# Hybrid decoder step: the linear attention's decay products on GpSimd ahead of the levels, with the order of all engines written out

## The chip, the cores and the metric

One core of a Trainium2 chip runs the whole step in one launch. Its engines work side by side, each on its own queue in order: TensorE (PE, matmuls, with weight loads listed as PEld), VectorE (DVE), ScalarE (ACT), GpSimd (POOL) and SyncE (SP), which issues the DMA transfers. The metric is the device time of one launch in microseconds; lower is better.

## The reference

A one-layer decoder step for a prompt of 2048 tokens and for 64 sample tokens (8 sequences of 8). One input projection feeds two mixers and their gates; the output projection is added to the residual. Mixer A is sliding-window attention in three windows and dilations, for the prompt and, with a cache, for the sample. Mixer B is gated linear attention with 4 heads, key size 64 and value size 128:

```python
def step(state, xs):
    qc, kc, vc, gc = xs
    b = jnp.cumsum(gc, axis=2)
    diff = b[:, :, :, None, :] - b[:, :, None, :, :]
    decay = jnp.exp(jnp.where(causal[:, :, None], diff, -jnp.inf))
    scores = jnp.einsum('bhtk,bhsk,bhtsk->bhts', qc, kc, decay)
    o = (jnp.einsum('bhts,bhsv->bhtv', scores, vc)
         + jnp.einsum('bhtk,bhkv->bhtv', qc * jnp.exp(b), state))
    b_last = b[:, :, -1]
    state = (jnp.exp(b_last)[..., None] * state
             + jnp.einsum('bhsk,bhsv->bhkv', kc * jnp.exp(b_last[:, :, None] - b), vc))
    return state, o
```

`gc` is the logarithm of a forget factor for each token, head and key channel. A score between two tokens carries the product of the factors between them.

## The kernel before

The prompt is cut into 16 tiles of 128 tokens. Each is normalised, transposed and multiplied by the input weights, block of columns by block of columns (`acc_q`, `acc_k`, `acc_v`, `acc_qkb`, `acc_g`, `acc_vb`, `acc_gb`; inputs and weights are split into two float16 parts, and each 128 rows of the weights take three matmuls). The windowed attention runs beside the projections. Then come the linear attention, while the last block of columns (`acc_gb`, the gate of mixer B) is still projected, and the output projection `Y`, beside which the sample's attention over the cache (`OS`) runs to the end.

The linear attention of the prompt works in eight blocks of 256 tokens (`e0` to `e7`; two chunks of 128 in each), one of the sample (`smp`) before them. `gla_core` does one block. Keys and queries are transposed to channels on partitions (`kq_e`: `kT` and `qT`, 128 x 2 x 256 numbers, flattened to 512 columns `k` and `q`), and so are the forget factors, `d_e`. Scores are then made by doubling: at level B (1, 2, 4, 8, 16, 32, 64; for the sample the first three) each pair of neighbouring spans of B tokens gets the scores of its later queries against its earlier keys. For that the later queries must carry the decay from the start of their span and the earlier keys the decay to the end of theirs. One level is:

- ACT copies the later queries into a zero-padded tile `qbd` (three tiles in turn, L840), PE makes the score products `sc_e` (L881; at level 64 L865), and VectorE writes them under a mask into `Ac_e` (L887);
- `decay()` then multiplies the earlier keys by the later span's whole factor on GpSimd (L848) and the later queries by the earlier span's whole factor on VectorE (L852). After it, every span of 2B tokens is decayed as one;
- the whole factors of the doubled spans, needed by the next level, are the products of neighbours (L858), half as many at each level: 256, 128, 64, 32, 16, 8 and 4 columns for a block of the prompt.

The keys of a level can only be decayed when the level's score products have read them, and the next level's products need the decayed keys: a chain of PE and GpSimd. The queries make a second one of ACT and VectorE. The last product of a block, the decay over a whole chunk, is read again by the state's update (`Sbd`, L1940). The tiles `d` and `sums` have two buffers each.

Around it on VectorE stand the normalisation of the outputs (`oss_c`, `rv_o_c`, `ra_o_c`, `ors_c`), the gate (`so_gb`, L1303 and L1311) and the mixing with the windowed attention (`oc`, `mn`, `mix`, `mt`); on GpSimd `prod_e`, `Ac_e` (L789), `gw` (L1395), `oc` (L2149) and the sample's dot products `pr` (L1616).

The order of each engine's instructions is fixed before the launch. A class `Plan` reads all instructions, finds their dependencies, prices each, and makes a list schedule by priorities; two tables of numbers in the kernel then change some priorities (`steps`) and move some rows (`shifts`). The result is given to the framework as the order in which each engine must run; the framework adds the semaphores.

Of the kernel before, what the change touches and what calls it, by code (L numbers as in the profile page):

```python
# [51 lines left out]
class Plan:  # L52

    ENGINES = ("PE", "DVE", "Activation", "Pool", "SP")

    def __init__(self, tc, nc, cross=35.0, traffic=1.0, lanes=8, room=212832):

        self.tc, self.cross, self.traffic = tc, cross, traffic
        self.lanes, self.room = lanes, room
        self.window, self.least = 3413.0, 0.5  # L60
        self.turns = ((0.0, 93.0, 93.0), (93.0, 0.0, 195.0), (93.0, 60.0, 0.0))
        traced = nc.cur_bb.bb.instructions
        self.at = {i.name: n for n, i in enumerate(traced)}
        self.ins = [
            i for i in traced
            if type(i).__name__ not in ("BassTilePoolBoundary", "InstTileManualSchedule")
        ]
        self.eng = [str(i.engine).split(".")[-1] for i in self.ins]
        self.bits, self.pools = {}, {p.id: p for p in tc.info.pools}
        self.read()  # L70
        self.depend()
        self.price()

    def mask(self, ap, dims, nbytes, row):

        key = (tuple(dims), ap.offset, nbytes, row)
        m = self.bits.get(key)
        if m is not None:
            return m

        def places(start, dims):
            idx = [start]
            for step, n in dims:
                if n > 1 and step:
                    idx = [i + step * j for j in range(n) for i in idx]
            return idx

        m = 0
        if row:
            p0, col = divmod(ap.offset, row)  # L90
            last = col + sum(step * (n - 1) for step, n in dims[1:])
            lo, hi = col * nbytes // 4, (last * nbytes + nbytes - 1) // 4
            line = (1 << (hi + 1)) - (1 << lo)
            width = row * nbytes // 4 + 1
            for q in range(p0 // 32, (p0 + dims[0][1] - 1) // 32 + 1):
                m |= line << (q * width)
        else:
            dims, run = list(dims), 1
            while dims and (dims[-1][0] == run or dims[-1][1] == 1):
                run *= dims.pop()[1]  # L100
            span = (1 << ((run + 15) // 16)) - 1
            for e in set(places(ap.offset, dims)):
                m |= span << (e // 16)
        self.bits[key] = m
        return m

    def read(self):

        self.acc, self.tile = [], {}
        for i in self.ins:  # L110
            acc = []
            for aps, w in ((i.ins, False), (i.outs, True)):
                for a in aps:
                    ap = getattr(a, "bass_ap", None)
                    if ap is None or getattr(ap.tensor, "cap_key", None) is None:
                        continue
                    t = ap.tensor
                    size = {F16: 2, BF16: 2}
                    nbytes = size.get(a.dtype, 4)
                    row = 0  # L120
                    if t.space != DRAM:
                        row = 1
                        for s in list(t.shape)[1:]:
                            row *= s
                        row = row * size.get(t.dtype, 4) // nbytes
                    m = 1 if t.space == PSUM else self.mask(
                        ap, [tuple(x) for x in a.ap], nbytes, row
                    )
                    acc.append((t.name, w, m))
                    self.tile.setdefault(t.name, t)  # L130
            if type(i).__name__ == "InstCopyPredicated":
                acc += [(t, False, m) for t, w, m in acc if w]
            self.acc.append(acc)

    def spans(self):

        end = len(self.at)
        events = []
        for p in self.pools.values():
            if p.space == DRAM:  # L140
                continue
            a = self.at[p.alloc_inst.name]
            r = p.release_inst and self.at.get(p.release_inst.name)
            events.append((a, 1, p))
            if r:
                events.append((r, 0, p))
        events.sort(key=lambda e: e[:2])
        stacks, slots = {}, {}
        for at, opens, p in events:
            st = stacks.setdefault((str(p.space), str(p.side)), [])  # L150
            if not opens:
                st[:] = [s for s in st if s[0] != p.id]
                continue
            lo = top = max((s[1] for s in st), default=0)
            for tag, meta in p.tag_meta.items():
                size = (meta.max_size_bytes // P + 31) // 32 * 32
                for j in range(meta.bufs):
                    slots[f"{tag}_{p.name}_{p.id}", j] = (str(p.space), str(p.side), top, top + size)
                    top += size
            st.append((p.id, top))  # L160
        for k, (space, side, lo, hi) in slots.items():
            if "right" in side.lower():
                lo, hi = self.room - hi, self.room - lo
            slots[k] = (space, lo, hi)
        return slots

    def depend(self):

        slots = self.spans()
        dep = [set() for _ in self.ins]  # L170
        behind = [set() for _ in self.ins]
        gates = []

        def gate(before):
            before = frozenset(before)
            if before:
                gates.append(before)
                return {len(self.ins) + len(gates) - 1}
            return set()

        whole = {}
        for n, acc in enumerate(self.acc):
            for t, _, _ in acc:
                whole.setdefault(t, []).append(n)

        of_pool, room = {}, {}
        for t, tile in self.tile.items():
            if tile.space != DRAM:
                of_pool.setdefault(str(tile.tag).rsplit("_", 1)[1], []).append(t)
        for (key, _), (space, lo, hi) in slots.items():  # L190
            i = key.rsplit("_", 1)[1]
            sp, l0, h0 = room.get(i, (space, lo, hi))
            room[i] = space, min(lo, l0), max(hi, h0)
        opens = {}
        for p in self.pools.values():
            i = str(p.id)
            if i not in room:
                continue
# [12 lines left out]
        for n, acc in enumerate(self.acc):  # L211
            for t, w, m in acc:
                if t in hist:
                    continue
# [2384 lines left out]
```

## Time and profile before

| | us |
|---|---|
| three runs: median (lowest to highest) | 1244.23 (1243.79 to 1245.26) |
| profiled execution, its own time | 1242.09 |
| its span, from first to last instruction | 1240.2 |
| PE busy | 1188.2 (96%) |
| VectorE busy | 947.9 (76%) |
| ScalarE busy | 820.6 (66%) |
| GpSimd busy | 545.1 (44%) |

The granted TensorE clock was 0.999 of full speed on the mean. Busy times of engines overlap. A row of a group gives its line, engine, operation, tiles, sizes and count, then its busy time and the mean of one in ns, then the idle time of the engine just before it and what ended that. "A <- B" in a table of waits means that A stood still until B was done. The ends of matmuls are modelled, so a gap of a few hundredths of a microsecond on PE isn't seen.

### The profile page before, as it was taken

To read this page: it belongs to the slowest core of one execution; us is meant where nothing else is said; L and a number is where in the kernel's file an instruction comes from. 1 tells how busy PE (TensorE), PEld (TensorE's weight loads), DVE (VectorE), ACT (ScalarE), POOL (GpSimd) and SP (SyncE) were. 2 spreads that over 40 slices of the span, in tenths; PEclk is the share of its full clock that TensorE was granted. 3 is DMA by queue.
4 is the path that set the end of the run, shared out by engine and by line. 5 is a ranking of instruction groups with operands and counts; after the bars stand their busy time and mean duration, and the time that the engine had idled before them with its cause. 6 is when DMAs were issued, how large, how long until landed. Compare 5 with 4: busy or idle time off the path is not lost.

```text
span 1240.2 us, 26200 instructions
## 1 busy us (share of the span) xinstructions
PE 1188.2 (96%) x8942; PEld 716.7 (58%) x8942; DVE 947.9 (76%) x2450; ACT 820.6 (66%) x2191; POOL 545.1 (44%) x475
## 2 busy tenths in 40 slices
PE   5999999999999999999999999999999999999998
PEld 3444564666566556666677665545655665555543
DVE  7988788988898958668677665589999999833662
ACT  6554697889689968968767653568878864411220
POOL 0154442575647334552444466655635454501220
PEclk9999999999999999999999999999999999999999
DMA  8668947986856898789999886865772477899971
GB/s 298 231 172 237 241 131 167 245 226 184 203 169 164 213 250 282 229 245 248 257 260 256 247 229 212 231 196 174 233 249 95 156 245 235 279 379 349 399 267 49
DMA packets 235831, 283.07 MB, mean 228 GB/s; under 512 B 116193, under 2 KB 146866, under 8 KB 232626
## 3 DMA queue, kind: packets, MB, share of 16 engines
q1 hardware_dynamic: 235698, 281.40, 75.8%
q8 instruction: 71, 1.16, 0.4%
q14 instruction: 62, 0.51, 0.1%
HBM read 183.02 MB, written 75.24 MB: 208 GB/s over the span
## 4 chain that ended last, share of the span: by engine, by line
PE 51%; DVE 19%; DMA 9%; ACT 8%; issue 5%; POOL 5%; SPq 1%; POOLq 0%; DVEq 0%; ACTq 0%
PE Y L2107 10%; PE acc_qkb L1761 4%; PE acc_gb L1761 4%; PE acc_v L1761 3%; PE t L1052 3%; PE acc_k L1761 3%; PE s L1034 3%; POOL pr L1616 3%; PE O L1067 3%; PE acc_q L1761 3%; PE acc_g L1761 2%; PE acc_vb L1761 2%; DMA k<-in_cache_k_win 2%; PE OS L2364 2%; DVE p L1042 2%
## 5 line engine op out<-in xcount | busy, mean ns | idle before, releaser
L1616 POOL TENSOR_TENSOR pr<-k,qb 128x512 f32<-128x512 f32 x128 | 168.3, 1315 | 171.1 <-DVE sck L1617 70.2
L1761 PEld LDWEIGHTS <-hr 128*128 128x128 f16 x1824 | 172.5, 98 | 110.9 <-issue 11.1
L1045 ACT ACTIVATE p<-p,o 128x256 f32<-128x256 f32 (+1 forms) x384 | 173.1, 455 | 22.9 <-DVE o L1042 20.2
L1761 PEld LDWEIGHTS <-hl 128*128 128x128 f16 x1248 | 119.7, 98 | 118.6 <-issue 7.0
L2107 PE MATMUL Y<-w_o,mh 128*128 128x512 f16 x768 | 180.4, 379 | 0.1
L1067 PE MATMUL O<-v,pt 128*128 128x128 f16 x1200 | 135.1, 220 | 7.9 <-DVE pt L1015 2.6
L1019 POOL TENSOR_TENSOR pt<-p,pt 128x512 f16<-128x512 f32 (+1 forms) x80 | 91.1, 1138 | 116.5 <-ACT pt L1018 92.0
L1617 DVE TENSOR_REDUCE sck<-pr 128x8 f32<-128x512 f32 x128 | 87.1, 680 | 56.7 <-POOL pr L1616 56.5
L1052 PE MATMUL t<-ident,p 128*128 128x128 f32 x600 | 119.2, 279 | 5.5 <-ACT p L1045 3.0
L2107 PEld LDWEIGHTS <-mh 128*128 128x128 f16 x768 | 72.3, 98 | 79.0 <-issue 5.6
L1067 PEld LDWEIGHTS <-pt 128*128 128x128 f16 x1200 | 94.6, 99 | 39.9 <-DVE pt L1015 4.6
L1761 PE MATMUL acc_v<-w_v,hl 128*128 128x512 f16 x384 | 110.0, 383 | 1.1 <-DVE vp L1416 1.0
L1761 PE MATMUL acc_g<-w_g,hr 128*128 128x272 f16 (+1 forms) x768 | 109.3, 276 | 1.4 <-DVE so_g L1303 1.4
L1761 PE MATMUL acc_q<-w_q,hl 128*128 128x512 f16 x384 | 109.5, 379 | 0.5 <-DVE vp L1416 0.5
L1761 PE MATMUL acc_k<-w_k,hl 128*128 128x512 f16 x384 | 108.7, 379 | 0.9 <-DVE vp L1416 0.9
L1761 PE MATMUL acc_vb<-w_vb,hr 128*128 128x512 f16 x384 | 95.3, 379 | 0.3 <-DVE so_g L1303 0.3
L1042 DVE CUSTOM_DVE_ANT_0 p<-s,m3w,scl_s 128x128 f32<-128x128 f32 (+1 forms) x256 | 87.2, 395 | 9.0 <-PE s L1034 5.1
L1761 PE MATMUL acc_gb<-w_gb,hr 128*128 128x512 f16 x384 | 93.8, 380 | 0.0
L1052 PEld LDWEIGHTS t<-ident,p 128*128 128x128 f32 x600 | 74.2, 141 | 28.4 <-ACT p L1045 14.1
L1034 PE MATMUL s<-kk,qq 128*128 128x256 f16 (+1 forms) x512 | 84.7, 264 | 4.4 <-DVE o L1042 2.3
L1761 PE MATMUL acc_qkb<-w_qkb,hr 128*128 128x512 f16 x288 | 81.5, 379 | 1.5 <-ACT zq L1381 1.5
L2149 POOL TENSOR_TENSOR oc<-oc 128x512 f32<-128x512 f32 x32 | 40.1, 1270 | 88.4 <-DVE oc L2142 69.4
(538 smaller groups left out, 2502.2 us busy)
## 6 DMA issues: line engine op xcount, KB each, us to landing
k<-in_cache_k_win SPq DMA_DIRECT2D x104, 256.0 KB
sv_b<-in_cache_v_win SPq DMA_DIRECT2D x24, 1024.0 KB
hr<-h_d SPq DMA_DIRECT2D x44, 512.0 KB
qb<-q_d SPq DMA_DIRECT2D x64, 256.0 KB
oc<-o_d SPq DMA_DIRECT2D x48, 264.0 KB
o_d<-o SPq DMA_DIRECT2D x64, 132.0 KB
x<-in_x_prompt SPq DMA_DIRECT2D x16, 512.0 KB
h_d<-hl SPq DMA_DIRECT2D x16, 512.0 KB
```

Source lines behind the costliest of these rows:

```text
L1019: POOL.tensor_tensor(l, f, h, ALU.subtract)
L1034: PE.matmul(s_ps[:, i * w : (i + 1) * w], q, k, start=(n == 0), stop=(n == len(prods) - 1),)
L1042: DVE.tensor_tensor_reduce(s[:, sl], s_ps[:, sl], mask, neg, BIG, ALU.add, ALU.min, nmf(i))
L1045: ACT.activation(s[:, sl], s[:, sl], AF.Exp, bias=nmf(i), scale=-1.0, accum_out=denf(i))
L1052: PE.transpose(p_ps[:, i * P : (i + 1) * P], t["s"][:, i * P : (i + 1) * P], ident[:])
L1067: PE.matmul(o_, t["pt"][:, c, (i * nb + b) * P : (i * nb + b + 1) * P], vf(i, b), start=(n == 0), stop=(n == 2 * nb - 1),)
L1616: POOL.tensor_tensor(pr[:], kt, qt, ALU.mult)
L1617: DVE.tensor_reduce(out, pr[:].rearrange("p (u k d) -> p u k d", u=2, k=4), AX.X, ALU.add)
L1761: PE.matmul(z, a_[:, k, :], w[:, p_, k, cols], start=(k == 0 and i == 0), stop=(k == KT - 1 and i == 2),)
L2107: PE.matmul(Y[:], a_[:, k, :], w_[:, part, k, :512], start=(i == 0), stop=(i == len(prods) - 1),)
L2149: eng.tensor_tensor(o_[g], o_[g], w[:, g].unsqueeze(2).to_broadcast([P, NH, HD]), ALU.mult)
L2364: PE.matmul(OS[32 * x : 32 * x + 32, 0:256], ps(x), vs_[bb][:, 256 * u : 256 * u + 256], start=(i == 0), stop=(i == 13),)
```

## The change

In `gla_core` the products of neighbours leave `decay()`. They are made by GpSimd instead of VectorE, and all levels of a block are made in one loop, before the first level's copy of queries; `wholes` keeps them, and level number `li` reads `wholes[li]`. The numbers computed are the same.

```diff
         sums = gt.tile([P, 2 * n], F32, name=f"sums_{tagp}", tag="sums", bufs=2)
-        whole, free = d[:], 0
+        wholes, free = [d[:]], 0
+        for B in levels:
+            M = n // B
+            part = wholes[-1].rearrange("p (m two) -> p m two", two=2)
+            wholes.append(sums[:, free : free + M])
+            free += M
+            POOL.tensor_tensor(wholes[-1], part[:, :, 0], part[:, :, 1], ALU.mult)
 
         yield
         for li, B in enumerate(levels):
...
-            part = whole.rearrange("p (m two) -> p m two", two=2)
+            part = wholes[li].rearrange("p (m two) -> p m two", two=2)
 
             def decay():
-                nonlocal whole, free
                 POOL.tensor_tensor(
                     kv[:, :, 0, :], kv[:, :, 0, :], part[:, :, 1:2].to_broadcast([P, M, B]),
                     ALU.mult,
                 )
...
-                whole = sums[:, free : free + M]
-                free += M
-                DVE.tensor_tensor(whole, part[:, :, 0], part[:, :, 1], ALU.mult)
...
-        return qT, kT, whole.rearrange("p (a m) -> p a m", a=2), Ac
+        return qT, kT, wholes[-1].rearrange("p (a m) -> p a m", a=2), Ac
```

The class `Plan` and the tables `steps` and `shifts` are removed. In their place stands, for each engine, the list of its instructions' numbers (as they are written in the program) in the order in which they run:

```diff
+ORDER = {
+    "PE": (
+        "6-7 0 2-4 1 5 10-25 8-9 74 90-91 75 92-93 76-77 94-99 78 100-113 79-89 26-33 42-49 34-41 50-65 "
...
+def in_order(tc, nc):
+
+    traced = {e: [] for e in ORDER}
+    for i in nc.cur_bb.bb.instructions:
+        if type(i).__name__ not in ("BassTilePoolBoundary", "InstTileManualSchedule"):
+            traced[str(i.engine).split(".")[-1]].append(i)
+    info = mybir.DependencyInfo(mybir.DependencyClass.NoSync, mybir.DependencyReason.DATA)
+    for e, runs in ORDER.items():
+        ends = [[int(n) for n in r.split("-")] for r in runs.split()]
+        order = [traced[e][n] for r in ends for n in range(r[0], r[-1] + 1)]
+        assert len(order) == len(traced[e])
+        for a, b in zip(order, order[1:]):
+            tc.add_manual_dep(b, a.name, info, reason="listed order")
...
-    plan = Plan(tc, nc)
...
-    order = plan.settle(3, 800.0, 1.15, 60.0, 10.0, steps)
-    plan.fix(plan.shift(order, shifts))
+    in_order(tc, nc)
```

The listed order is mostly the planned one: of PE's 13,534 rows of instructions some 98% stand in the same sequence. It differs where the products were and are, in the linear attention around them, and by short moves in the rest of the program: a few matmuls of a projection earlier or later than a transpose beside them, a DMA issue ahead of another on SP, a copy on ACT before or after its neighbour. For block `e3`, PE's score products of level 1 stand ahead of the gate projection of tiles 7 to 9 instead of near its end. The rows that show the moved products on VectorE and GpSimd stand in the prediction. Line numbers after the change are smaller by 134, in the loop over levels by 130 or 131: L840 becomes L710, L848 L717, L852 L721, L865 L731 and L881 L747; the products' L858 becomes L701.

More of the change, by code (lines that the diff above doesn't have):

```diff
@@ new lines @@
+ORDER = {
[266 rows of a table added]
+    ),
+    "DVE": (
[81 rows of a table added]
+    ),
+    "Activation": (
[72 rows of a table added]
+    ),
+    "Pool": (
[19 rows of a table added]
+    ),
[43 rows of a table added]
+    ),
+}
+def in_order(tc, nc):
[10 more added lines that the diff above has]
+            tc.add_manual_dep(b, a.name, info, reason="listed order")
@@ L2499, in tile_hymba @@
-    plan = Plan(tc, nc)
-    steps, shifts = (
-        [tuple(int(v) for v in s.split(":")) for s in some.split()] for some in (steps, shifts)
-    )
-    order = plan.settle(3, 800.0, 1.15, 60.0, 10.0, steps)
-    plan.fix(plan.shift(order, shifts))
+    in_order(tc, nc)
 _INS = [
```

666 lines of the change are left out of this document (removed), and 479 rows, old and new, of the table ORDER.

## The prediction

> **What bounds the kernel now.** I read the page first, then the busy time by stage, then TensorE's own waits in the stage that the change touches, then the order of time at one of those waits. The page's first part says which engine to look at:
>
> ```profile
> PE 1188.2 (96%) x8942; PEld 716.7 (58%) x8942; DVE 947.9 (76%) x2450; ACT 820.6 (66%) x2191; POOL 545.1 (44%) x475
> ```
>
> TensorE (PE) is busy in 1188.2 us of a span of 1240.2, so all of its waiting together is 52 us, and no edit that leaves its matmuls alone can win more than that. The stages, cut where the work changes (columns: PE, weight load, VectorE = DVE, ScalarE = ACT, GpSimd = POOL), show where those 52 us lie:
>
> ```profile
> 0.00:60.00 60.00, 43.39 (x237) 21.88 (x238) 51.07 (x124) 38.84 (x66) 4.07 (x10) 1.00 0.76 260
> 60.00:780.00 720.00, 697.58 (x5153) 446.26 (x5151) 557.68 (x1532) 534.42 (x1579) 367.04 (x303) 1.00 0.82 220
> 780.00:820.00 40.00, 37.44 (x230) 21.84 (x228) 25.42 (x46) 25.20 (x57) 21.28 (x19) 1.00 0.87 255
> 820.00:900.00 80.00, 76.97 (x631) 44.77 (x629) 75.58 (x181) 63.19 (x155) 45.50 (x46) 1.00 0.59 192
> 900.00:960.00 60.00, 59.22 (x489) 33.08 (x488) 54.73 (x132) 50.55 (x116) 26.68 (x28) 1.00 0.52 172
> 960.00:1020.00 60.00, 59.49 (x495) 36.93 (x495) 56.91 (x137) 45.34 (x101) 27.62 (x27) 1.00 0.58 195
> 1020.00:1080.00 60.00, 58.34 (x432) 33.62 (x431) 53.85 (x142) 27.80 (x67) 28.17 (x27) 1.00 0.75 246
> 1080.00:1205.00 125.00, 124.94 (x1133) 64.94 (x1131) 62.24 (x147) 30.86 (x53) 24.76 (x21) 1.00 0.92 356
> ```
>
> The linear attention of the prompt runs from about 780 to 1080 us. There PE is idle for 2.56 + 3.03 + 0.78 + 0.51 + 1.66 = 8.5 us, which is the ceiling of what the moved products can win. Behind it, from 1080 to 1205, PE never waits (124.94 of 125): time won ahead of it moves the end as it stands, and nothing there gives more. VectorE is the next bound: in 820 to 1080 it is busy for 75.58 + 54.73 + 56.91 + 53.85 = 241.1 of 260 us (93%), GpSimd for 128.0 (49%). What PE waits for in 780 to 1085 (engine, line waited for: us, times, longest):
>
> ```profile
> PE sc_e L881 <- POOL kq_e L848: 2.2, 3, 1.1
> PE sc_e L881 <- ACT qbd L840: 1.9, 4, 0.9
> PE pg_e L812 <- ACT kq_e L809: 1.4, 1, 1.4
> PE tm L2072 <- DVE Ac_e L887: 1.2, 1, 1.2
> PE ptg_e L804 <- DVE la_e L825: 0.7, 1, 0.7
> PE u_e L816 <- ACT gT_e L813: 0.5, 1, 0.5
> PE O L1927 <- ACT ob_c L925: 0.4, 1, 0.4
> ```
>
> Half of it, 4.1 us, is the level products `sc_e` waiting for decayed keys (POOL, L848) or for the copy of decayed queries (ACT L840, behind DVE L852). The other rows are single waits.
>
> **The change, part by part: what leaves VectorE.** For each of the eight blocks seven products at L858, and three for the sample. By size (busy us and mean ns), then their spread (minimum/median/maximum ns):
>
> ```profile
> L858 DVE TENSOR_TENSOR sums_e<-sums_e 128x128 f32<-128x128 f32 x8 | 5.1, 637 | 0.0
> L858 DVE TENSOR_TENSOR sums_e<-d_e 128x256 f32<-128x256 f32 x8 | 4.2, 525 | 0.0
> L858 DVE TENSOR_TENSOR sums_e<-sums_e 128x16 f32<-128x16 f32 x8 | 4.2, 524 | 0.0
> L858 DVE TENSOR_TENSOR sums_e<-sums_e 128x64 f32<-128x64 f32 x8 | 3.9, 483 | 0.0
> L858 DVE TENSOR_TENSOR sums_e<-sums_e 128x8 f32<-128x8 f32 x8 | 2.8, 352 | 0.0
> L858 DVE TENSOR_TENSOR sums_e<-sums_e 128x4 f32<-128x4 f32 x8 | 2.7, 341 | 0.0
> L858 DVE TENSOR_TENSOR sums_e<-sums_e 128x32 f32<-128x32 f32 x8 | 2.5, 312 | 0.0
> ...
> L858 DVE TENSOR_TENSOR sums_e<-sums_e x48: 147/208/2123, 821.2 to 1045.9; 128x128 f32<-128x128 f32 x8, 128x64 f32<-128x64 f32 x8, 128x32 f32<-128x32 f32 x8, 128x16 f32<-128x16 f32 x8
> L858 DVE TENSOR_TENSOR sums_e<-d_e x8: 412/419/1072, 819.5 to 1028.7; 128x256 f32<-128x256 f32 x8
> ```
>
> The seven rows add up to 25.4 us, a tenth of VectorE's 241.1. By the medians the work itself is 48 x 0.208 + 8 x 0.419 = 13.3 us; the other 12 us is stretch. What stretches them shows in the order of time (start us, us), VectorE's rows, then GpSimd's, then PE's:
>
> ```profile
> 821.21 2.05 DVE L858 TENSOR_TENSOR sums_e<-sums_e 128x128 f32<-128x128 f32 x1
> 824.71 1.28 DVE L858 TENSOR_TENSOR sums_e<-sums_e 128x64 f32<-128x64 f32 x1
> ...
> 821.22 1.88 POOL L2001 TENSOR_TENSOR vx<-vb_s,bm 64x1024 f32<-64x1024 f32 x1
> 824.53 1.38 POOL L1616 TENSOR_TENSOR pr<-k,qb 128x512 f32<-128x512 f32 x1 [1.43 <-DVE sck L1617]
> ...
> 831.96 1.26 POOL L1395 TENSOR_TENSOR gw_s<-so_gbs,gnw 64x512 f32<-64x512 f32 x1 [5.06 <-DVE ra_o_smp L767]
> 833.19 0.73 POOL L848 TENSOR_TENSOR kq_e<-kq_e,sums_e 128x256 f32<-128x256 f32 x1
> ...
> 833.98 0.69 PE L881 MATMUL sc_e<-qbd,kq_e 128*64 128x64 f32 x16 [1.05 <-POOL kq_e L848]
> ```
>
> A product of 128 columns took 2.05 us, ending with GpSimd's `vx` of 1.88 us that ran beside it; the next ended with `pr`. And this lateness is what PE pays for: GpSimd's `gw_s` stood 5.06 us waiting for VectorE, the keys' decay stood behind it on GpSimd, and PE waited 1.05 us for that decay. The two products cost VectorE 3.3 us between 821 and 832; without them `gw_s` and the decay start up to 3.3 us sooner, and the wait of 1.05 is covered. What is late next there is the copy of the queries, whose waits of at most 0.9 us hang on VectorE too.
>
> [...]
>
> The order on VectorE at the first block (`e0`; `sc_e0_1` is level 1's score, `kq_e0` keys and queries, `za_0`, `la_e2`, `so_gbs` other work). Before:
>
> ```order
> L887 COPY_PREDICATED Ac_e0_10019<-gmask_9590,sc_e0_1_10056 128x256
> L1617 TENSOR_REDUCE sck_7_7896<-pr_3_7_3_8558 128x2x4
> L858 TENSOR_TENSOR sums_e0_10053<-d_e0_10050 128x256
> L1463 TENSOR_TENSOR za_0_12748<-za_0_12748,acc_gb_s_12731 64x512
> L852 TENSOR_TENSOR kq_e0_10021<-kq_e0_10021,sums_e0_10053 128x128x2
> L858 TENSOR_TENSOR sums_e0_10053<-sums_e0_10053 128x128
> L825 SCALAR_TENSOR_TENSOR la_e2_11060<-u_e2_11057,la_e2_11060 128x512
> ```
>
> and after, at the same place:
>
> ```order
> L1329 TENSOR_TENSOR za_0_12753<-za_0_12753,acc_gb_s_12736 64x512
> L753 COPY_PREDICATED Ac_e0_10019<-gmask_9590,sc_e0_1_10063 128x256
> L721 TENSOR_TENSOR kq_e0_10021<-kq_e0_10021,d_e0_10050 128x256
> L1483 TENSOR_REDUCE sck_7_7896<-pr_3_7_3_8558 128x2x4
> L721 TENSOR_TENSOR kq_e0_10021<-kq_e0_10021,sums_e0_10053 128x128x2
> L689 SCALAR_TENSOR_TENSOR la_e2_11060<-u_e2_11057,la_e2_11060 128x512
> ```
>
> Both products are gone from between the query decays, and a level's decay no longer waits for a product that stands behind other work.
>
> **What comes onto GpSimd.** No run shows a product there; its nearest rows are the keys' decays (by form: busy us, mean | idle before) and their spread:
>
> ```profile
> L848 POOL TENSOR_TENSOR kq_e<-kq_e,sums_e 128x256 f32<-128x256 f32 x48 | 33.6, 701 | 46.5 <-PE sc_e L881 27.2 <-PE sc_e L865 6.2 <-issue 4.5
> L848 POOL TENSOR_TENSOR kq_e<-kq_e,d_e 128x256 f32<-128x256 f32 x8 | 8.0, 998 | 11.7 <-PE sc_e L881 11.6
> L848 POOL TENSOR_TENSOR kq_smp<-kq_smp,sums_smp 128x64 f32<-128x64 f32 x2 | 0.6, 314 | 1.9 <-DVE gmax_a L1311 1.0 <-POOL kq_smp L848 1.0
> ...
> L848 POOL TENSOR_TENSOR kq_e<-kq_e,sums_e x48: 614/642/1149, 833.2 to 1053.3; 128x256 f32<-128x256 f32 x48
> L848 POOL TENSOR_TENSOR kq_e<-kq_e,d_e x8: 839/844/1879, 818.6 to 1026.4; 128x256 f32<-128x256 f32 x8
> ```
>
> 256 columns take 0.64 to 0.84 us, 64 take 0.31. A line through 0.314 at 64 and the higher of the two has a slope of 2.8 ns and 0.14 us at zero; through the lower, 1.7 ns and 0.2 us. So the seven are, with an estimate between the lines, about 0.75 + 0.45 + 0.31 + 0.25 + 0.22 + 0.2 + 0.2 = 2.4 us a block (the lines give 2.4 and 2.3), 19 us for eight, and about 0.8 for the sample's three. The means of the same rows, 0.70 and 1.00, hold the waiting for VectorE as well; with a third more for that it is 3.2 us a block. They lie beside the wait that GpSimd has anyway: it is idle for half of the stage, 58 us of it in front of the decays themselves. Where this cover is gone, ahead of a block's first decay, is shown by block `e6`. Before, GpSimd had:
>
> ```order
> L848 TENSOR_TENSOR kq_e5_12646<-kq_e5_12646,sums_e5_12678 128x8x32
> L848 TENSOR_TENSOR kq_e5_12646<-kq_e5_12646,sums_e5_12678 128x4x64
> L848 TENSOR_TENSOR kq_e6_13581<-kq_e6_13581,d_e6_13610 128x256
> L1395 TENSOR_TENSOR gw_15_13777<-so_gb15_13770,gnw_394 128x512
> L848 TENSOR_TENSOR kq_e6_13581<-kq_e6_13581,sums_e6_13613 128x128x2
> ```
>
> and now:
>
> ```order
> L717 TENSOR_TENSOR kq_e5_12646<-kq_e5_12646,sums_e5_12678 128x4x64
> L701 TENSOR_TENSOR sums_e6_13613<-d_e6_13610 128x256
> L701 TENSOR_TENSOR sums_e6_13613<-sums_e6_13613 128x128
> L701 TENSOR_TENSOR sums_e6_13613<-sums_e6_13613 128x64
> L701 TENSOR_TENSOR sums_e6_13613<-sums_e6_13613 128x32
> L701 TENSOR_TENSOR sums_e6_13613<-sums_e6_13613 128x16
> L701 TENSOR_TENSOR sums_e6_13613<-sums_e6_13613 128x8
> L701 TENSOR_TENSOR sums_e6_13613<-sums_e6_13613 128x4
> L717 TENSOR_TENSOR kq_e6_13581<-kq_e6_13581,d_e6_13610 128x256
> L1261 TENSOR_TENSOR gw_15_13783<-so_gb15_13776,gnw_394 128x512
> ```
>
> All seven stand between two decays. They wait for `d_e6` from ACT and for the second of two `sums` buffers; behind them on GpSimd stand the first decay and `gw_15`, and PE's level 2 waits for that decay. The other blocks are mixed: `e0` has its seven among the sample's dot products, well ahead.
>
> **The rest of the order.** Some dozens of short moves on PE, ACT, VectorE and SP lie outside this stage, none of more than a few instructions. PE's idle time there is 16.6 us in the first 60 and 22.4 us up to 780. Of the first, most is one wait:
>
> ```profile
> PE mx_v L1203 <- DVE w_v L1260: 14.6, 1, 14.6
> ```
>
> It ends with VectorE's reductions of the first weights, all of which still stand ahead of it. I price these moves at -0.5 us, between -3 and +2: each touches single waits of about a microsecond.
>
> **The sum,** against the profiled execution's own 1242.09 us (span 1240.2, 1.9 around it), which lies 2.1 below the median of 1244.23. The 4.1 us of `sc_e` waits: two thirds go, -2.7. The waits for VectorE and ACT at `tm` and `O`, 1.2 + 0.4: -1.0. The three waits ahead of the first block (1.4 + 0.7 + 0.5), which precede the products: -0.6, by VectorE's relief alone. The other moves: -0.5. New waits where products precede a first decay: +0.5. Together -4.3: 1237.8 for a profiled execution, 1239.9 for the median. Bounds of this course: all 8.5 us and the 3 elsewhere, 1232.7; nothing won and a little lost, 1245. Its own likely range is 1235 to 1242.
>
> **Rivals.** First, slower: GpSimd becomes the late one. The row of first decays shows 11.7 us of idle before eight of them, 1.46 us a block, against 2.4 us of products; the excess is 0.95 us a block, and if PE has no other matmul ready there it pays 8 x 0.95 = 7.6 us, while perhaps 1.5 of the gains stay: +6, 1250.3. It decides where `d_e` comes less than 2.4 us ahead of the first decay's turn. For it: seven in a row at `e6`. Against it: most blocks have their products spread or far ahead, and the gate projection's matmuls can fill. Second, no change: GpSimd's 19 us hold VectorE up in turn. If every microsecond of them blocks it, VectorE gets back 25.4 - 19 = 6 us, and of 4.3 us gained about 1 is left: 1243.2. Against it: the products are short, and the 12 us of stretch that their own rows show on VectorE go with them. Third, more: the moves elsewhere recover several of the 22.4 us as well; with 3 more and 2 more from the stage, 1235.
>
> **How the numbers follow.** 0.2%, about 2.5 us, is what a measurement of this kernel can tell from no change. Forecast 0.50, more 0.12, both faster: 0.62. No change 0.15. Slower 0.23. The range reaches from below the third rival, 1233.5, to 1249, just under the first rival's price, which leaves out some two in ten.
>
> **What would show it.** Right: the L858 rows gone from VectorE, whose busy time from 820 to 1080 falls by 13 to 25 us; about 20 us more on GpSimd; PE's waits for `kq_e` and `qbd` under 2 us; the stage from 780 to 1080 shorter by 3 to 5 us and 1080 on unchanged. Wrong: PE waiting longer for `kq_e` with the products ahead of it on GpSimd; VectorE's two-input instructions stretched by as much as was removed; or a gain that lies before 780, where no product was moved.

## The result, and the profile after

| | before | after |
|---|---|---|
| median of 22 runs each on one chip, us | 1241.48 | 1245.29 |
| ratio to before [95% interval] | | 1.0029 [1.0017, 1.0040] |
| profiled execution, its own time (span) | 1242.09 (1240.2) | 1243.81 (1241.9) |

The changed kernel is slower by 0.29%, some 3.6 us. The forecast was 0.35% faster; the range reached up to 1249 and held the time, the direction was wrong. (Ratios, and the medians further down, leave disturbed runs out: one of 1371 us of the kernel before, one of run E3 and two of run C3.) The profiled pair differs by 1.7 us only, so its traces hold less than half of the difference of the medians.

The page's first part, and then the stages up to 1080 us as in the prediction (PE, weight load, DVE, ACT, POOL busy us, then granted clock):

```profile
PE 1189.4 (96%) x8942; PEld 716.7 (58%) x8942; DVE 930.0 (75%) x2391; ACT 820.5 (66%) x2191; POOL 568.4 (46%) x534
```

```profile
0.00:60.00 60.00, 42.44 (x232) 21.44 (x233) 50.31 (x122) 38.59 (x64) 2.92 (x9) 1.00 0.74 256
60.00:780.00 720.00, 699.32 (x5164) 447.34 (x5162) 551.41 (x1532) 534.94 (x1581) 369.83 (x307) 1.00 0.82 220
780.00:820.00 40.00, 38.17 (x228) 21.46 (x227) 25.02 (x45) 23.44 (x54) 23.81 (x26) 1.00 0.88 264
820.00:900.00 80.00, 77.84 (x653) 46.42 (x651) 68.14 (x163) 63.62 (x155) 53.93 (x66) 1.00 0.60 190
900.00:960.00 60.00, 58.70 (x470) 31.90 (x469) 49.57 (x116) 51.48 (x117) 31.52 (x42) 1.00 0.52 171
960.00:1020.00 60.00, 57.79 (x485) 35.76 (x484) 57.41 (x124) 44.20 (x98) 30.59 (x33) 1.00 0.59 192
1020.00:1080.00 60.00, 57.75 (x425) 33.04 (x423) 53.47 (x133) 27.48 (x67) 29.57 (x32) 1.00 0.72 233
```

TensorE's idle time shrank where the stage begins (780 to 900: 5.6 to 4.0 us) and grew behind it: 0.8 to 1.3 up to 960, 0.5 to 2.2 up to 1020, 1.7 to 2.3 up to 1080. What it waits for longest from 940 to 1040, after (before it was `qbd` alone, 0.7 us):

```profile
PE sc_e L747 <- ACT qbd L710: 1.2, 2, 0.7
PE O L1793 <- DVE Sbd L1806: 1.0, 1, 1.0
PE u_e L680 <- ACT gT_e L677: 0.5, 1, 0.5
```

The other two are of 0.2 us, and none is for a key decay: TensorE's last wait for `kq_e` lies ahead of 940. The longest single one is `O`, which reads the state `Sbd` that VectorE updates. Around it, in order of time (VectorE, then TensorE, then GpSimd):

```profile
973.33 0.41 DVE L721 TENSOR_TENSOR kq_e<-kq_e,sums_e 128x256 f32<-128x256 f32 x1
...
973.99 1.05 DVE L1806 SCALAR_TENSOR_TENSOR Sbd<-Sbd,sums_e,U 64x128 f32<-64x128 f32 x3
974.97 0.88 DVE L1151 SCALAR_TENSOR_TENSOR w_o<-wr_o,ns_o,w_o 128x512 f16<-128x512 f32 x1
975.88 0.35 DVE L1806 SCALAR_TENSOR_TENSOR Sbd<-Sbd,sums_e,U 64x128 f32<-64x128 f32 x1
...
976.28 0.70 PE L1793 MATMUL O<-Sbd,kq_e 128*128 128x256 f32 x2 [1.04 <-DVE Sbd L1806]
...
976.38 1.05 POOL L701 TENSOR_TENSOR sums_e<-d_e 128x256 f32<-128x256 f32 x1 [1.08 <-DVE Sbd L1806]
...
980.53 1.19 POOL L717 TENSOR_TENSOR kq_e<-kq_e,d_e 128x256 f32<-128x256 f32 x1 [0.42 <-PE sc_e L747]
```

and before, at the same place:

```profile
974.83 1.42 DVE L1940 SCALAR_TENSOR_TENSOR Sbd<-Sbd,sums_e,U 64x128 f32<-64x128 f32 x4
976.29 1.13 DVE L1285 SCALAR_TENSOR_TENSOR w_o<-wr_o,ns_o,w_o 128x512 f16<-128x512 f32 x1
...
976.49 0.65 PE L1927 MATMUL O<-Sbd,kq_e 128*128 128x256 f32 x2
```

Two things stand here side by side. The list puts a weight column `w_o` ahead of the fourth state update and the last query decay ahead of all four, and TensorE pays 1.04 us. Without that wait `O` would have begun at 975.2, ahead of before's 976.5: what goes here is a lead that TensorE had. And GpSimd's first product of `e6` waits 1.08 us for the same update, since that update reads the `sums` buffer of `e4`, which `e6` writes anew; on VectorE the product stood behind the update anyway. Here that second wait costs nothing by itself: behind all seven products the first decay still waits 0.42 us for TensorE. What the products cost GpSimd, by form:

```profile
L701 POOL TENSOR_TENSOR sums_e<-d_e 128x256 f32<-128x256 f32 x8 | 6.8, 854 | 4.3 <-ACT d_e L691 2.2 <-DVE Sbd L1806 1.9
L701 POOL TENSOR_TENSOR sums_e<-sums_e 128x128 f32<-128x128 f32 x8 | 5.3, 659 | 0.3
L701 POOL TENSOR_TENSOR sums_e<-sums_e 128x64 f32<-128x64 f32 x8 | 3.1, 392 | 0.3
L701 POOL TENSOR_TENSOR sums_e<-sums_e 128x8 f32<-128x8 f32 x8 | 2.3, 287 | 0.5
L701 POOL TENSOR_TENSOR sums_e<-sums_e 128x32 f32<-128x32 f32 x8 | 1.9, 240 | 0.6
L701 POOL TENSOR_TENSOR sums_e<-sums_e 128x16 f32<-128x16 f32 x8 | 1.9, 239 | 0.5
L701 POOL TENSOR_TENSOR sums_e<-sums_e 128x4 f32<-128x4 f32 x8 | 1.6, 201 | 0.5
```

22.9 us, or 2.9 a block, and 1.9 us of waiting for `Sbd`.

### The profile page after: what moved, and what is told of

Same layout as the page of the kernel before. It is cut to its first block, busy times and chain, and to the rows that moved or that the text cites. A ratio compares the mean times of both kernels' runs of the same rounds, so it can differ in the third digit from the quotient of the medians.

```text
span 1241.9 us, 26183 instructions
## 1 busy us (share of the span) xinstructions
PE 1189.4 (96%) x8942; PEld 716.7 (58%) x8942; DVE 930.0 (75%) x2391; ACT 820.5 (66%) x2191; POOL 568.4 (46%) x534
```

## The experiments

The change has two parts that can be taken apart, since both kernels trace the same instructions but for the products: where the products are made, and each engine's order. "Before's order" below is the planner's order written out as a list. (The list of TensorE has 8019 rows, of which 7867 keep before's sequence.) All kernels ran in five rounds beside the kernel before. Ratios are to it, in brackets the 95% interval; "own tile" and "idle" are explained at their runs. Runs have capital names (E1), blocks small ones (`e1`).

| run | products | order | median us (before) | ratio |
|---|---|---|---|---|
| changed kernel | GpSimd | listed | 1245.3 (1241.4) | 1.0029 [1.0017, 1.0040] |
| E1 | GpSimd | before | 1243.9 (1241.0) | 1.0021 [1.0008, 1.0035] |
| E2 | VectorE | listed | 1253.4 (1241.0) | 1.0102 [1.0078, 1.0125] |
| E3 | GpSimd | listed to 740 | 1245.9 (1241.0) | 1.0038 [1.0022, 1.0055] |
| E4 | GpSimd | listed from 740 | 1243.3 (1241.0) | 1.0017 [1.0000, 1.0035] |
| B4 | VectorE | listed to 740 | 1242.9 (1241.3) | 1.0008 [0.9994, 1.0022] |
| B1 | GpSimd to `e4`, then VectorE | before | 1240.7 (1241.3) | 0.9997 [0.9986, 1.0007] |
| B2 | GpSimd, own tile | before | 1241.2 (1241.3) | 0.9995 [0.9982, 1.0008] |
| B5 | GpSimd, own tile, idle | before | 1242.4 (1241.3) | 1.0013 [1.0000, 1.0026] |
| C1 | GpSimd, own tile | listed | 1246.0 (1240.6) | 1.0028 [1.0008, 1.0049] |
| C2 | GpSimd, own tile, idle, last late | listed from 740 | 1242.7 (1240.6) | 1.0011 [0.9993, 1.0030] |
| C3 | as C2 | before | 1238.4 (1240.6) | 0.9980 [0.9958, 1.0002] |
| D1 | as B1, own tile | before | 1239.4 (1240.6) | 0.9980 [0.9961, 0.9999] |
| F1 | GpSimd | listed to 940 | 1243.7 (1241.7) | 1.0023 [1.0007, 1.0039] |
| F2 | VectorE | listed 940 to 1085 | 1247.8 (1241.7) | 1.0035 [1.0020, 1.0050] |
| F3 | as C2 | listed 750 to 940 | 1240.9 (1241.7) | 0.9996 [0.9983, 1.0010] |
| F4 | as C2, `e7` on VectorE | before | 1239.4 (1241.7) | 0.9987 [0.9973, 1.0002] |
| G1 | GpSimd | listed, one row back | 1242.8 (1241.3) | 1.0008 [0.9990, 1.0025] |
| G2 | GpSimd | listed, VectorE from 940 as before | 1244.1 (1241.3) | 1.0021 [1.0005, 1.0038] |

The medians lie close, so each trace was also set against that of before: at which time had TensorE done the same amount of matmul work? The table gives by how much each fell behind (+) or gained (-) in two stretches of before's time; (h) marks a stretch that holds a half-clock window (last section), worth about 1.7 us. In plain idle time from 940 to 1040 the changed kernel's TensorE loses 2.8 us (0.9 before, 3.7 after), not 4.0. What the table has beyond the idle time, 0.5 to 1.3 us in all kernels that follow the list somewhere between 750 and 1085, is matmul work that took longer or stands in another sequence; on before's order the two measures agree to 0.2 us, with 1.7 us for a marked window.

| us | changed | E1 | E2 | E4 | B1 | B2 | B5 | C1 | C3 | D1 | F1 | F2 | F3 | G1 | G2 |
|---|---|---|---|---|---|---|---|---|---|---|---|---|---|---|---|
| 780 to 940 | -1.8 | -0.6 | +2.7 (h) | -2.0 | -1.1 | -2.2 | -1.9 | -2.3 | -2.6 | -2.4 | -1.8 | -0.4 | -2.2 | -2.5 | -2.0 |
| 940 to 1040 | +4.0 | +4.0 (h) | +6.4 | +3.9 | -0.1 | +2.3 | +2.1 | +4.7 | +0.9 | -0.1 | +5.2 (h) | +6.5 (h) | +2.3 | +3.1 | +3.4 |

**Each half alone.** E1 keeps every other row at before's place; E2 makes the products on VectorE again, at their old places among their neighbours or up to a dozen rows earlier where the moved rows need them.

```diff
 # E1, from the changed kernel
-ORDER = listed
+ORDER = before's, with the products on GpSimd in front of the same neighbours as listed
 # E2, from the changed kernel (ORDER = listed)
-            POOL.tensor_tensor(wholes[-1], part[:, :, 0], part[:, :, 1], ALU.mult)
+                DVE.tensor_tensor(whole, part[:, :, 0], part[:, :, 1], ALU.mult)      # in decay()
```

> All other instructions of all engines stand in the order of before; only the 59 products are moved to GpSimd, each in front of the same neighbour as in the changed kernel. If the products on GpSimd are what costs (theory A: GpSimd becomes the late engine in the last blocks), this is as slow as the changed kernel, 3 to 5 us above before (1244.5 to 1246.5). If the re-ordering is what costs (theory B), the products alone gain or are neutral: 1238 to 1241.5. If only the two together cost (theory C), it is within 1 us of before.

> The products stay on VectorE, level by level; every other instruction stands in the listed order of the changed kernel. Theory A (products cost): not slower than before, 1239 to 1242. Theory B (the re-ordering costs): 1245 or more, 3 to 5 us above before, since VectorE still has the products' 25 us. Theory C: within 1 us of before.

Both are slower than before: theory C falls, and neither A nor B is enough. The products alone cost 0.21%; the list without them costs 1.02% (six runs): its VectorE rows were set without the products, which had to be put back among them.

**The order up to 740 us.** Spliced lists; B4 has the products on VectorE.

```diff
 # E3, B4: ORDER = listed up to about 740 us, before's from there
 # E4:     ORDER = before's up to about 740 us, listed from there
```

> Products on GpSimd as in the changed kernel; the listed order up to the sample's block of the linear attention (about 740 us), before's order from there. In the profiled pair the early part gained 0.6 us up to 780 and the loss of 3.1 us lay between 958 and 1100. Theory A: like the changed kernel, 1244.5 to 1246. Theory B with the cost in the late order: 1238 to 1241. Theory B with the cost in the early order: 1244 to 1246, and more than the run with the early order of before.

> Products on GpSimd; before's order up to about 740 us, the listed order from there. Theory A: 1244.5 to 1246. Theory B, late order: 1244.5 to 1246. Theory B, early order: 1240 to 1242.

> Products on VectorE, no product moved; the listed order up to about 740 us, before's order from there. The two pairs of runs that differ in the early order alone put it at +1.8 us: if that holds, 1242 to 1244 against before's 1241; if it was scatter of the runs, 1240.5 to 1241.5.

E3 came out where theory A has it, E4 (1243.3) between that and theory B's 1240 to 1242. Three pairs differ in the early list alone: E3 over E1 (+0.17%), the changed kernel over E4 (+0.12%), B4 over before (+0.08%). All point one way, by 1 to 2 us, and none of the three is clear of zero by its interval; this part stays open.

**What the products cost.** B1 moves those of `e5` to `e7` back to VectorE. B2 gives each prompt block's last product, the one that the state's update reads, a small tile, so that `sums` is free as soon as the block's decays are done. B5 moves in addition the products of `e5` and `e7` to where GpSimd stood idle.

```diff
+AHEAD = ("smp", "e0", "e1", "e2", "e3", "e4")     # B1: these on GpSimd, the others in decay() on VectorE
...
-        sums = gt.tile([P, 2 * n], F32, name=f"sums_{tagp}", tag="sums", bufs=2)      # B2, B5
+        sums = gt.tile([P, 2 * n - 8], F32, name=f"sums_{tagp}", tag="sums", bufs=2)
...
-            wholes.append(sums[:, free : free + M])
+            if B == 64:
+                last = gt.tile([P, 4], F32, name=f"last_{tagp}", tag="last", bufs=2)
+                wholes.append(last[:])
+            else:
+                wholes.append(sums[:, free : free + M])
```

> Order of before; products on GpSimd ahead of the levels for the sample and blocks e0 to e4 as in the run with the products alone, on VectorE level by level as before for e5 to e7. In the run with the products alone TensorE gained about 1.7 us on before between 780 and 900 and lost 4 us between 940 and 1040. If that loss comes from the products of e5 to e7 on GpSimd (theory A), this keeps the gain and drops the loss: 1238.5 to 1240.5, against 1241 of before. If it comes from anything that the first blocks' products do, or is spread evenly, 1242 to 1244.

> As the run with the products alone, but each block's last product, which the state's update reads, gets a small tile of its own, so that the next products but one no longer wait for that update on VectorE. Theory A1 (that wait delays the products of e5 and e6 by 0.8 to 1.1 us each): 1 to 2 us faster than the products alone (1242 to 1243). Theory A2 (the products' own 2.9 us in front of the first decay): unchanged, 1243.5 to 1244.5. [...]

> As the run with the last product in a tile of its own, with the seven products of e5 moved ahead of the gate product gw in front of which GpSimd idles 3 us, and those of e7 ahead of the mixing product oc in front of which it idles 3.8 us. Theory A (products stand in the way of the first decays): the loss between 940 and 1040 mostly goes, 1239 to 1241. [...]

Either edit, B1 or B2, takes the 0.2% away; E1's interval (from 1.0008) and theirs (up to 1.0007 and 1.0008) barely touch. In E1, GpSimd before `e4`'s first decay, then `e7`'s; then the product of B2 for `e4`:

```profile
930.56 0.61 POOL L724 TENSOR_TENSOR sums_e<-d_e 128x256 f32<-128x256 f32 x1 [2.94 <-ACT osq_c L807]
931.13 0.85 POOL L740 TENSOR_TENSOR kq_e<-kq_e,d_e 128x256 f32<-128x256 f32 x1
...
1023.78 2.43 POOL L724 TENSOR_TENSOR sums_e<-sums_e 128x128 f32<-128x128 f32 x4
...
1027.41 0.82 POOL L724 TENSOR_TENSOR sums_e<-sums_e 128x8 f32<-128x8 f32 x2
1028.19 0.84 POOL L740 TENSOR_TENSOR kq_e<-kq_e,d_e 128x256 f32<-128x256 f32 x1
```

```profile
928.29 0.88 POOL L728 TENSOR_TENSOR sums_e<-d_e 128x256 f32<-128x256 f32 x1
```

At `e4` the product stood 2.94 us; the profile names `osq_c`, but the wait is gone once the last product has its own tile, so it was for the buffer's readers. TensorE paid for it: from 900 to 940 it idles 1.5 us in E1, all of it for that decay, and not at all in B2. At `e7` there is no such wait: products of 3.3 us simply stand ahead of the first decay (1028.19, against the 1026.4 at which the last such row of before starts), and TensorE waits for it in E1 and in B2 alike. E1's waits for a key decay from 900 to 940, then from 940 to 1040:

```profile
PE sc_e L770 <- POOL kq_e L740: 1.5, 1, 1.5
...
PE sc_e L770 <- POOL kq_e L740: 1.8, 1, 1.8
```

B5 missed its forecast. Its `last` tiles are two as well, and the last product now stood ahead of the work that frees its tile:

```profile
947.31 2.30 POOL L728 TENSOR_TENSOR sums_e<-sums_e 128x128 f32<-128x128 f32 x5
952.30 0.37 POOL L728 TENSOR_TENSOR last_e<-sums_e 128x4 f32<-128x4 f32 x1 [2.69 <-DVE Sbd L1833]
952.63 2.26 POOL L1288 TENSOR_TENSOR gw<-so_gb,gnw 128x512 f32<-128x512 f32 x1
954.86 0.79 POOL L744 TENSOR_TENSOR kq_e<-kq_e,sums_e 128x256 f32<-128x256 f32 x1
955.61 0.84 POOL L744 TENSOR_TENSOR kq_e<-kq_e,d_e 128x256 f32<-128x256 f32 x1
```

The wait was moved, not removed: 2.69 us for `Sbd`, with `gw` and both decays behind it. The same happens at `e7` (2.75 us), where TensorE's wait for the decay is still 1.1 us.

**The same cures on both orders.** C2 and C3 have B5's places, but each last product directly in front of its block's last key decay.

```diff
 # C1: the changed kernel            + B2's tile
 # C2: E4                            + B2's tile, B5's places, last products late
 # C3: E1                            + B2's tile, B5's places, last products late
 # D1: B1                            + B2's tile
```

> The changed kernel with one edit: each block's last product in a small tile of its own, so that the first six products of the next block but one no longer wait for the state's update. Theory A1 (the wait for the shared buffer is what the change costs; in the changed kernel's trace GpSimd stands 0.8 us at e5 and 1.1 us at e6 for it): 1.5 to 3 us faster than the changed kernel's 1245.3, 1242 to 1243.5, still above before by the 1.5 us of the early order. Theory A2 (only the products' own time in front of the decays): unchanged, 1244.5 to 1245.5.

> Before's order up to about 740 us, the listed order from there, last products in a tile of their own and directly in front of the block's last key decay, the first six of e5 and e7 in front of a gate product and a mixing product before which GpSimd idles. If the wait for the buffer (A1) and the products in front of the first decay of e7 (A2) are the whole loss between 940 and 1040, this runs 3 to 4 us faster than the same order without them (1243.3): 1238.5 to 1240.5, faster than before. If the move only shifts the wait, 1242 to 1243.

> The same placing of products on before's order everywhere. In the run with the products in the idle time the last product still stood 2.7 us for the state's update with the gate and mixing products behind it; here the last product comes late. If that wait was what kept that run at 1242.4, this gives 1239 to 1240.5; if products on GpSimd cost VectorE as much as they relieve it there, 1241 to 1242.

> The run with e5 to e7 on VectorE, with the last products in a tile of their own. In its trace 1.1 us was lost between 900 and 940 where block e4's products stand in front of its first decay and wait for the update of e2: if the tile takes that away, 1239 to 1240 against 1240.7; if not, unchanged.

On before's order the products now seem to pay: C3 and D1 run 0.20% below before, D1 just clear of zero and C3 not (F4 below, much like them, 0.13%); against the changed kernel's 1.0029 that is half a per cent. On the listed order the tile brings nothing (C1), and the loss behind 940 stays: A1, which explains E1, does not explain the changed kernel. C1's waits there still hold the 1.0 us for `Sbd` and 1.2 for `qbd`, so freeing GpSimd frees nobody.

These runs also price the order where it was meant to stand, with the products on GpSimd. C1 and B2 have the same program and the tile, and differ in the order: C1 is slower by 0.33%, between 0.09 and 0.57 by the two intervals together. C2 and C3 differ in the order from 740 on: 0.31%, between 0.02 and 0.60. Between the changed kernel and E1, where the buffer's wait is in both, it is 0.08% and not clear of zero.

**The listed order of `e5` to `e7`.**

```diff
 # F1: the changed kernel, ORDER from about 940 us on = before's (products as in E1)
 # F2: the kernel before,  ORDER from about 940 to 1085 us = listed (products on VectorE)
 # F3: C3, ORDER from about 750 to 940 us = listed
 # F4: C3, products of e7 on VectorE
```

> The changed kernel, with before's order of all engines from about 940 us on (blocks e5 to e7 and after). Theory O (the listed order of e5 to e7 costs 4 us by itself, and the products about 2 on before's order there): 1.5 to 2.5 us faster than the changed kernel's 1245.3, at 1242.5 to 1244. Theory G (GpSimd's products in the last blocks cost it whatever the order): unchanged, 1244.5 to 1246.

> The kernel before, products on VectorE, with the listed order only between about 940 and 1085 us. Theory O: 2 to 5 us slower than before, 1243 to 1246, with the loss between 940 and 1040. Theory G (the listed order is harmless, it only shows the products' cost): within 1 us of before.

> Products on GpSimd, last products in a tile of their own and late, the first six of e5 and e7 in idle time; the listed order only from about 750 to 940 us, before's elsewhere. Theory O: like the same placing on before's order or better, 1238 to 1239.5. If the listed order's stretch up to 940 is worth nothing beyond what the tile gives, 1239 to 1240. Theory G: 1242 or more.

> Before's order, products on GpSimd with the last ones in a tile of their own and late, those of e5 in idle time, those of e7 on VectorE. On the same order e7's products on GpSimd still cost 0.9 us between 1020 and 1040: 1238 to 1239.5, faster than before by 0.15 to 0.25%.

F2 comes out as theory O has it: on before's program the list of these 145 us alone costs 0.35%, as much as the whole change within the intervals. That is no price for the changed kernel, since the products are back on VectorE in a list set without them (the 0.9 us at `tm` are for one of them); C1 against B2 is nearer to that. F2's longest waits from 940 to 1040, none of which before has:

```profile
PE O L1817 <- DVE Sbd L1830: 1.0, 1, 1.0
PE u_e L706 <- ACT gT_e L703: 1.0, 1, 1.0
PE mx_o L1096 <- DVE mm_o L1095: 1.0, 1, 1.0
PE tm L1962 <- DVE sums_e L748: 0.9, 1, 0.9
```

F1 is no faster than the changed kernel within the intervals. Its trace shows why the two costs need not add: with before's order put back there, the products' own cost (1.9 us for `kq_e` at `e7`) comes in place of the list's. F3 (1240.9) came out above both of its better forecasts, F4 at the edge of its own; by them the list has no measurable worth up to 940 beyond what the tile gives, and `e7` on either engine is the same within the interval.

**Which row.** In the changed kernel, one exchange in VectorE's list (G1), or its whole list from 940 (G2):

```diff
 "DVE":                              # G1
-  ... 1444-1446 1549 1447 1568 ...  # Sbd Sbd Sbd w_o Sbd kq_e6
+  ... 1444-1447 1549 1568 ...       # Sbd Sbd Sbd Sbd w_o kq_e6
```

> The changed kernel with two neighbouring rows of VectorE exchanged: the fourth state update of e5 ahead of the weight column w_o instead of behind it. If that row is what TensorE and GpSimd wait for there, both waits of about 1 us at 975 go, and the loss between 960 and 980 falls by about 1 us: 1244 to 1245 against 1245.3, a difference that the time alone hardly resolves and the trace does. If the wait only moves to the next row, the loss between 940 and 1040 stays at 4 us.

> The changed kernel with VectorE's rows from about 940 us on in the order of before (without the products), all other engines as listed. If VectorE's list is what costs there: the loss between 940 and 1040 falls from 4 to 1 or 2 us, 1242.5 to 1244. If it is the lists of TensorE and ScalarE, it stays: 1245 to 1246.5.

(The update in question is `e4`'s, counting eight to a block; G1's expectation calls it `e5`'s.) G1's trace does what was forecast, and its time more (1242.8; by the trace the row is worth 0.9 us, and the rest is within the scatter). In order of time, and below it TensorE's wait:

```profile
975.74 1.42 DVE L1830 SCALAR_TENSOR_TENSOR Sbd<-Sbd,sums_e,U 64x128 f32<-64x128 f32 x4
977.19 0.75 DVE L1175 SCALAR_TENSOR_TENSOR w_o<-wr_o,ns_o,w_o 128x512 f16<-128x512 f32 x1
...
977.30 1.11 POOL L725 TENSOR_TENSOR sums_e<-d_e 128x256 f32<-128x256 f32 x1 [0.26 <-DVE Sbd L1830]
```

```profile
PE O L1817 <- DVE Sbd L1830: 0.2, 1, 0.2
```

TensorE's wait fell from 1.0 to 0.2 us, GpSimd's from 1.08 to 0.26. G2's time stays within the changed kernel's interval, but its trace divides the loss. TensorE from 960 to 1000 us, before, in the changed kernel and in G2 (busy us, then granted clock), and below that G2's longest wait up to 1040:

```profile
960.00:1000.00 40.00, 39.49 (x347) 1.00 0.51 167
960.00:1000.00 40.00, 37.88 (x338) 1.00 0.49 150
960.00:1000.00 40.00, 39.54 (x348) 1.00 0.51 168
```

```profile
PE Y L1997 <- DVE xr L2004: 1.6, 1, 1.6
```

With VectorE's rows as before, the 2.1 us of idle time here are down to 0.5, as before. At 1030 another wait comes in their place: before's list has `mix` ahead of `xr` on VectorE, and `mix` now waits 0.9 us for GpSimd's `oc`, which stands behind products of `e7`. The other traces agree. Those with VectorE's listed rows here (the changed kernel, C1, C2, E4, F2) idle 2.1 to 3.3 us in this stretch, G1 1.3, and all on before's rows 0.4 to 1.2 (E2, some 10 us late by then, can't be compared). So VectorE's rows hold this part of the loss, and setting them all back makes a new wait, as GpSimd has other work by then. Which rows it is besides G1's wasn't taken further.

## Why the prediction was wrong

By its own steps, with TensorE's waits from 780 to 1085 in the profiled pair:

- **What leaves VectorE, and what it gains.** The products went, and a part of the gain came: TensorE gained 1.6 us between 780 and 900. Over the stage its `sc_e` waits for `qbd` and `kq_e` fell from 4.1 to 3.1 us, against a forecast of 2.7 less. The waits at `tm` and `O`, of which 1.0 us was to go, stayed whole (`O` for `ob_c` 0.5 us), and the three ahead of the first block fell by 0.3 of the 0.6 us:

```profile
PE sc_e L747 <- ACT qbd L710: 1.6, 3, 0.7
PE sc_e L747 <- POOL kq_e L717: 1.5, 3, 0.8
PE tm L1938 <- DVE Ac_e L753: 1.2, 1, 1.2
```

  VectorE's busy time from 820 to 1080 fell by 12.5 us (241.1 to 228.6), just under the 13 to 25 expected. (The least of the products of 128 columns is 273 ns, against the 2.05 us of the one that ran beside `vx`.)
- **The price on GpSimd.** 2.9 us a block against the estimate of 2.4. Small, but in front of `e7` it counts whole.
- **"New waits where products precede a first decay: +0.5" is the first step that failed.** The prediction named both things it needed, the seven products in a row and the second `sums` buffer, and priced them as if other work covered them. On before's order they cost 0.21%: a wait of up to 2.9 us for the buffer's old readers, 1.5 us of it TensorE's (gone in B2), and 1.8 us of TensorE's time at `e7`. The buffer was no cost on VectorE, whose own queue held the reader and the writer in sequence; made on another engine, the same reuse became a wait between two engines. In the changed kernel's own trace the new waits come to 1.9 us (`O` for `Sbd` 1.0, `acc_gb` 0.4, two single ones at `sc_e` 0.5), and none of them is for a product or a key decay.
- **"The other moves: -0.5" is the second, and the larger in the changed kernel.** It placed the moves outside this stage. Ahead of 780 TensorE's idle time did fall, by 0.8 us in the profiled pair, though the runs of the early list point the other way. But the moves around `e5` to `e7` lie inside the stage and had no price: with the products on GpSimd and the buffer cured, the order costs 0.33% (C1 against B2), and TensorE loses 1.6 us more from 960 to 1000 in the changed kernel, on VectorE's rows (G2). A `w_o` column in front of one state update is a single row, and it stood in the order; it wasn't asked who waits for the row behind it.
- **The terms together.** -1.0, +0.1, -0.3 and +1.9 make 0.7 us lost in this stage, where -3.8 was forecast; the two spans differ by 1.7 us and the runs by some 3.6. What the profiled pair doesn't hold stays open but for the clock (last section).
- **The rivals.** Rival 1, GpSimd late, had the mechanism and its rule (where the input comes less than the products' time ahead of the first decay), but spread it over eight blocks; it holds at `e7` in E1, and with the buffer's wait at `e4`. In the changed kernel it doesn't show: TensorE's waits for `kq_e` fell from 2.2 to 1.5 us, and none lies behind 940. So the rival has the right direction for the changed kernel by luck, not by its mechanism. Rival 2, VectorE held up in turn, is borne out in part in VectorE's busy time and not in the kernel's. VectorE's busy time in the linear attention, 745 to 1085 (third number with its count), of before and of E1:

```profile
745.00:1085.00 340.00, 331.11 (x2516) 193.44 (x2515) 289.73 (x678) 227.34 (x525) 177.34 (x170) 1.00 0.65 209
```

```profile
745.00:1085.00 340.00, 329.18 (x2493) 192.15 (x2491) 279.49 (x617) 225.35 (x524) 198.57 (x229) 0.99 0.64 206
```

Some 26 us of products went, 25.4 of them in the blocks; on the same order VectorE is 10.2 us less busy. Added up one by one, the durations of its other instructions in this stretch rose by 9.9 us (304.0 to 313.9); the rest is that rows overlap less. That is no cost that the time shows: in B2 VectorE is as busy as in E1 (281.3 us), and the time is that of before. That every microsecond of GpSimd's products blocks VectorE, as rival 2 has it, is shown by no run: in E1 GpSimd is busy for 21.2 us more, and VectorE's other rows took those 9.9 us longer.

No single cause carries the 0.29%. Shown, each at the edge of what these runs resolve: on before's order, products ahead of the decays (buffer and queue); with the products cured, the listed order. Curing one in the changed kernel lets the other come forward (C1, F1). Open: the early list, which rows beside G1's, and the part that the profiled pair doesn't hold.

## What to carry to other kernels

When work moves to another engine, look at the reuse of its buffers: a write that followed its old reader in one queue becomes a wait between engines, and everything behind it in the new queue waits too (here 2.94 us of GpSimd's time at `e4` in E1, and 1.5 us of TensorE's). Price an order by the row that each exchanged row is now ahead of and by who waits for that one; it is a cost of its own, here 0.33% on the division of work that it was written for and 1.02% on the other. And take a change of two parts apart before explaining it: here the one part was worth 0.1 to 0.2% once its waits were cured, hardly clear of zero, and stood hidden behind the other.

## What the hardware showed unexpectedly

In the clock records of the traces TensorE's granted clock drops to half for windows of 3.41 us: leaving out the last microseconds, every trace holds one to six of them, most often one near 570 us (568.87 to 572.28 before, 568.15 to 571.56 after), the others at different times in each. These two stand right behind waits of TensorE, which was busy for 62% and 70% of the 3.41 us ahead of them. So does one in E1, behind the 1.8 us at `e7`: the 3.41 us ahead of a window and the window itself (PE busy first, the clock third from the end):

```profile
1027.18:1030.59 3.41, 1.56 (x23) 1.12 (x23) 3.11 (x6) 2.08 (x5) 2.43 (x5) 1.00 0.38 110
1030.59:1034.00 3.41, 3.41 (x16) 1.76 (x14) 1.54 (x6) 1.71 (x3) 0.07 (x1) 0.50 0.99 298
```

TensorE was busy for 46% of the stretch ahead. Cut into such stretches of 3.41 us from the clock's first record on, all 20 traces together show where a window followed: behind all 9 in which TensorE was busy for less than 40%, behind 9 of 14 between 40 and 50%, behind 26 of 216 between 50 and 72%, and above that behind 1 of some 6700, which was itself at half speed. So a wait may cost twice: three of the four traces with 1.8 or 1.9 us of waiting at `e7` (E1, E3, F1, not B2) have a window right behind it, and a window of 3.41 us at half speed costs, by estimate, up to 1.7 us. That the waits bring the windows about wasn't tried by itself.

The mean granted clock was 0.9972 to 0.9977 for before in the different jobs (22 to 35 runs each), 0.9968 over the changed kernel's 22, 0.9950 over E2's 6 and 0.9982 over F4's 12. Times 1240 us, by estimate 0.5 to 1.1 of the 3.6 us lie there.
